# A 2048-token decoder trunk on one core: FFN input loaded eighth by eighth, weight sums moved ahead, and the loads of the down projection taken apart from their splits

## The chip, the cores and the metric

One NeuronCore of a Trainium2 chip. The metric is the time of one execution in microseconds of device time. The kernel before takes 2434.5 us, the median of three runs (2428.35, 2434.5 and 2436.43).

## The reference

One layer on a sequence of 2048 tokens, width 1024, in float32: an input projection that feeds two kinds of heads (gated mixing in chunks of 128 tokens, and a matrix memory carried from chunk to chunk), an output projection with a residual, a feed-forward block with a causal convolution of three taps behind its up projection, a gated input embedding, and a last norm. What the change touches is the feed-forward block:

```python
h = rms_norm(x, g_ffn[i])
up = causal_dwconv(h @ w_up[i], ffn_conv_w[i], ffn_conv_b[i])   # 1024 -> 5632
a, bv = jnp.split(up, 2, axis=-1)
x = x + (jax.nn.silu(a) * bv) @ w_down[i]                       # 2816 -> 1024
gate = jax.nn.sigmoid(rms_norm(x, g_ple[i]) @ w_ple_gate[i])
x = x + gate * (p[i] @ w_ple[i])
return rms_norm(x, g_final)
```

## The kernel before

Every float32 product is made of three TensorE (PE) products of a rounded high half and the rest: high x high, high x low, low x high. So each operand is first split: ACT copies the high half, DVE subtracts it from the whole. The functions `wsplit`, `halves` (L738) and `split` (L744) do that.

**Phase one** (up to L696) takes the tokens in four blocks of 512, one after the other, some 220 us each. A block runs four token groups (the value, gate and output-gate weights `w_v`), the query, key and gate tiles (`qk_tile`, `u_tile`), the heads, and the output projection. A `qk_tile` ends with a convolution on DVE (tile `cv`, L526), a SiLU on ACT (L528), and the head that follows begins with PE's products `pm` (L536). The block's sum with the residual goes to a buffer in HBM, `x1s[b]`. During block b, `make_h` of the block before brings that result back in four parts of 512 KB (tile `xs`, L694), multiplies it by the norm (L231), and stores the FFN input (`td`). The even blocks store two quarters a part; the odd ones also load the even block's (`hs`, L238) and store the sums and differences from which the feed-forward block makes its products: it multiplies 2x2 blocks of matrices with 7 block products in place of 8, in the order `ORDER = (1, 2, 6, 5, 7, 3, 4)`. The tiles `xs` come from a pool of two, which the streams of the block input `xT` use as well. The weights of the down projection need such sums too, 11 pairs of rows (`sums_load`, `sums_make`, L252 to L266: two loads of 512 KB into tiles `ds0` and `ds1`, four DVE operations, four stores to `sd`).

**Phase two** keeps its tiles in rings (`SLOTS`): 28 of kind "k" and 7 "r" of 4 KB a partition, 4 "f", 2 large "w", 8 small "m", 4 "x". A ring's next tile waits until the last use of the one that it replaces is over. It runs `up_half(0)`, `down_half(0)`, `up_half(1)`, `down_half(1)`, each for half the tokens, and then the embedding (`Ple`) for the four blocks. An up half has 22 columns j with 7 steps each, a down half 7 products with 11 steps each; a step is 12 PE products of 128x512. `Steps.run` calls functions a number of steps ahead of the step that uses them:

```python
early = [(4, lambda prod=prod, k=k: o.load(prod, k)), (2, lambda prod=prod, k=k: o.prep(prod, k))]
if k == NK - 1 and prod in (2, 7, 3, 4):
    early.append((2, lambda prod=prod: o.fetch(*{2: (0, 0), 7: (1, 1), 3: (0, 1), 4: (1, 0)}[prod])))
```

In a down half, `load` brings weights and activations into an "x" tile (`sx`, L915 and L916), `prep` splits them (`dw`, `dt`), `fetch` brings a residual quarter (`xr`, L924, 1 MB into a "w" tile). Down half 0 also makes the inputs of the second up half (`build_t`: `hx` loads of 512 KB into "x" tiles, split into `tt`); down half 1 does the same with the gate weights (`w_pg`, tile `wst`, L995) and the embedding's input (`xg`, L1007, into "f" tiles).

A tile scheduler works out the instruction streams: each engine runs its own in order, and where the code doesn't pin an instruction (`tc.keep_in_program_order`), the scheduler places it by its own estimate of when its inputs are there. Loads are issued on SP in order, most stores on POOL. A load that has to wait for its tile holds up every load behind it on SP.

## Time and profile before

| | |
|---|---|
| profiled execution | 2437.65 us, of which the span of the trace is 2435.9 |
| PE busy | 2352.9 us (97%) |
| DVE busy | 1813.4 us (74%) |
| ACT busy | 1101.5 us (45%) |
| DMA, mean of the span | 157 GB/s |
| phase one | 0 to 872 us, blocks end at about 220, 430 and 650 |
| up half 0, down half 0 | 872 to 1323, 1323 to 1544 us |
| up half 1, down half 1 | 1544 to 1967, 1967 to 2195 us |
| embedding and last norm | 2195 to 2436 us |

PE's busy time counts a product from its start to its modelled end, at whatever clock the chip granted. So what the kernel loses against an unbroken stream of products is its idle time plus the stretches at a lower clock. The granted clock is given for a stretch as its mean: 1.00 is the upper of two levels, 2.4 GHz, 0.50 the lower, 1.2 GHz.

### The profile page before, as it was taken

Reading aid. Unit: us, or ns where it says so; the run is one execution under the profiler, and the core shown is the slowest. Engines: PE = TensorE matmul, PEld = TensorE weight load, DVE = VectorE, ACT = ScalarE, POOL = GpSimd, SP = SyncE. Lnnn points to the kernel's source line nnn. Section 1 sums busy time; section 2 is a strip of 40 time slices with the busy share of each in tenths; the row PEclk is TensorE's granted clock in tenths of the full one; section 3 lists DMA queues with packets and bytes.
Section 4 is the critical chain, followed back from the end, with each engine's and each line's share of the span. In section 5 each row is a group of like instructions: output and inputs, shape, how many; then the busy total and the mean of one; then the engine's idle time right before and its main releaser. Section 6 shows DMA issues by size and latency. Waiting matters only on the chain.

```text
span 2435.9 us, 31412 instructions
## 1 busy us (share of the span) xinstructions
PE 2352.9 (97%) x11336; PEld 1990.2 (82%) x11336; DVE 1813.4 (74%) x3107; ACT 1101.5 (45%) x1848; POOL 206.3 (8%) x339
## 2 busy tenths in 40 slices
PE   8999999989999989999999999999999998999998
PEld 8888987988798868787788777788888877888887
DVE  7787767677766669898897657788888866575666
ACT  4453265246326554444444555444444444553323
POOL 1100100020010101011110000010100000000000
PEclk9999999999999999999999999999999999999999
DMA  7626533572543254355554777332332467671111
GB/s 252 228 94 198 159 98 119 163 238 78 165 136 98 87 208 149 120 183 197 179 189 159 252 251 261 140 108 100 122 124 101 134 223 245 206 258 53 70 70 70
DMA packets 145245, 382.72 MB, mean 157 GB/s; under 512 B 17344, under 2 KB 19520, under 8 KB 144064
## 3 DMA queue, kind: packets, MB, share of 16 engines
q1 hardware_dynamic: 118704, 291.16, 36.8%
q0 software_dynamic: 26240, 89.15, 9.4%
q8 instruction: 89, 1.46, 0.2%
q14 instruction: 68, 0.56, 0.1%
q10 hardware_dynamic: 144, 0.40, 0.1%
HBM read 283.12 MB, written 97.52 MB: 156 GB/s over the span
## 4 chain that ended last, share of the span: by engine, by line
PE 68%; DMA 11%; DVE 11%; issue 6%; ACT 2%; POOL 1%; SPq 1%; DVEq 0%; POOLq 0%; ACTq 0%
PE ub L827 4%; PE ub L828 4%; PE ub L829 4%; DMA hx<-td 4%; PE acc L125 4%; PE acc L124 4%; PE acc L127 4%; PE ua L827 3%; PE ua L828 3%; PE ua L829 3%; PE gt L124 3%; PE gt L125 3%; PE gt L127 3%; PE acc L371 3%; PE acc L373 3%
## 5 line engine op out<-in xcount | busy, mean ns | idle before, releaser
L827 PE MATMUL ub<-tt,sw 128*128 128x512 f32 x704 | 275.9, 392 | 9.7 <-ACT tt L740 5.6
L828 PE MATMUL ub<-tt,sw 128*128 128x512 f32 x704 | 275.7, 392 | 2.8 <-DVE tt L741 2.8
L829 PE MATMUL ub<-tt,sw 128*128 128x512 f32 x704 | 274.9, 391 | 0.0
L746 ACT ACTIVATE sw<-wr 128x1024 fp32r<-128x1024 f32 x132 | 140.0, 1061 | 286.0 <-PE ua L828 239.3
L827 PE MATMUL ua<-tt,sw 128*128 128x512 f32 x528 | 208.0, 394 | 9.7 <-DVE ua L857 9.0
L828 PE MATMUL ua<-tt,sw 128*128 128x512 f32 x528 | 207.2, 392 | 0.0
L829 PE MATMUL ua<-tt,sw 128*128 128x512 f32 x528 | 206.9, 392 | 0.0
L117 DVE TENSOR_TENSOR wlo<-wst,whi 128x1024 fp32r<-128x1024 f32 (+2 forms) x144 | 158.5, 1103 | 41.6 <-PE acc L127 22.9
L371 PE MATMUL acc<-whi,hh 128*128 128x384 f32 (+1 forms) x512 | 173.4, 339 | 9.1 <-ACT hh L217 6.7
L372 PE MATMUL acc<-wlo,hh 128*128 128x384 f32 (+1 forms) x512 | 172.7, 338 | 0.0
L747 DVE TENSOR_TENSOR sw<-wr,sw 128x1024 fp32r<-128x1024 f32 x132 | 161.0, 1220 | 15.1 <-ACT sw L746 12.3
L373 PE MATMUL acc<-whi,hl 128*128 128x384 f32 (+1 forms) x512 | 172.1, 337 | 0.2 <-DVE hl L218 0.2
L827 PEld LDWEIGHTS ub<-tt,sw 128*128 128x128 f32 x704 | 133.0, 189 | 41.1 <-ACT tt L740 6.5
L828 PEld LDWEIGHTS ub<-tt,sw 128*128 128x128 f32 x704 | 132.8, 189 | 31.1 <-DVE tt L741 4.0
L829 PEld LDWEIGHTS ub<-tt,sw 128*128 128x128 f32 x704 | 132.9, 189 | 27.7
L939 PE MATMUL da<-dt,dw 128*128 128x512 f32 x352 | 140.0, 398 | 9.0 <-DVE dt L741 9.0
L938 PE MATMUL da<-dt,dw 128*128 128x512 f32 x352 | 138.9, 396 | 4.2 <-ACT dt L740 4.2
L741 DVE TENSOR_TENSOR dt<-sx,dt 128x512 fp32r<-128x512 f32 x154 | 105.9, 688 | 47.9 <-ACT dt L740 47.6
L741 DVE TENSOR_TENSOR dw<-sx,dw 128x512 fp32r<-128x512 f32 x154 | 105.8, 687 | 46.2 <-ACT dw L740 45.9
L940 PE MATMUL da<-dt,dw 128*128 128x512 f32 x352 | 139.0, 395 | 0.0
L740 ACT ACTIVATE dw<-sx 128x512 fp32r<-128x512 f32 x154 | 95.9, 623 | 82.0 <-DMA sx<-w_down 27.6
L740 ACT ACTIVATE dt<-sx 128x512 fp32r<-128x512 f32 x154 | 96.1, 624 | 70.2 <-PE db L940 31.8
(339 smaller groups left out, 5737.5 us busy)
## 6 DMA issues: line engine op xcount, KB each, us to landing
wr<-w_up SPq DMA_DIRECT2D x44, 512.0 KB, 3.7
wr<-w_up SPq DMA_DIRECT2D x88, 256.0 KB, 4.9
act<-fc POOLq DMA_DIRECT2D x44, 512.0 KB, 5.7
ad<-two POOLq DMA_DIRECT2D x88, 256.0 KB, 4.9
sx<-sd SPq DMA_DIRECT2D x88, 256.0 KB, 4.1
sx<-ad SPq DMA_DIRECT2D x88, 256.0 KB, 4.3
wst<-w_v SPq DMA_DIRECT2D x48, 384.0 KB, 3.2
sx<-w_down SPq DMA_DIRECT2D x66, 256.0 KB, 4.4
```

The costliest lines, as they stand in the source:

```text
L124: PE.matmul(ps, wh, mh, start=(i == 0), stop=False)
L125: PE.matmul(ps, wh, ml, start=False, stop=False)
L127: PE.matmul(ps, wl, mh, start=False, stop=(i == n - 1))
L371: PE.matmul(ps[t][:, :n], a_h, rh, start=(k == 0), stop=False)
L372: PE.matmul(ps[t][:, :n], a_h, rl, start=False, stop=False)
L373: PE.matmul(ps[t][:, :n], a_l, rh, start=False, stop=(k == KD - 1))
L740: A.activation(t[:, :HALF], x, AF.Copy)
L741: V.tensor_tensor(t[:, HALF:], x, t[:, :HALF].bitcast(F32), ALU.subtract)
L747: V.tensor_tensor(lo, x, hi.bitcast(F32), ALU.subtract)
L827: PE.matmul(ps, hi[:, c], t[:, :HALF], start=first, stop=False, skip_group_check=on)
L828: PE.matmul(ps, hi[:, c], t[:, HALF:], start=False, stop=False, skip_group_check=on)
L829: PE.matmul(ps, lo[:, c], t[:, :HALF], start=False, stop=last, skip_group_check=on)
```

## The change

The FFN input of a block is now loaded and made in separate functions, each called for one of the four parts (`ffn_load`, `ffn_make`), spread by `ffn_at` over token group 2 and 3 and the tiles behind. It goes through the tiles `ds0` (the block's result) and, in odd blocks, `ds1` (the even block's quarters), of which there is one each and which the weight sums use as well. All 11 weight sums are made in phase one (`SUMS_T`, `turn`); the five in up half 0 are gone. In the down halves, the loads of `hx` go into "m" tiles, 256 KB each and 4 steps ahead, the residual into two "f" tiles, 4 steps ahead, the gate weights into "f" tiles, 5 steps ahead, and the embedding's input of even blocks into "w" tiles, 9 steps ahead; their splits are pinned at their step. The embedding's loads for the next block are called at tile 3, the splits at tile 6.

```diff
+SUMS_T = {1: 0, 2: 1, 3: 2, 0: 3}
...
             for i in range(2):
                 ST.dma_start(t[1 + i][:, kk, :], xs[:, i, :])
             return
-        hs = pair()
-        for i in range(2):
-            DMA.dma_start(hs[:, i, :], t[1 + i][:, kk, :])
         ST.dma_start(t[3][:, kk, :], xs[:, 1, :])
         t5, t7, t6, t4 = one(), one(), one(), one()
         V.tensor_tensor(t7, xs[:, 1, :], xs[:, 0, :], ALU.subtract)
...
             rB = nq.rB
+            if b == NB - 1:
+                sums_load(SUMS_T[0], ds_tile)
 
...
                 nx.st1()
 
+            if b == NB - 1:
+                sums_make(SUMS_T[0])
+            if b:
+                sums_load(SUMS_T[b], ds_tile)
             ps = tok_group(1, {0: [chain1], 1: [chain2], 2: [chain3]} | ({3: [pend[0].st2]} if b else {}))
...
+            if 0 < b:
+                sums_make(SUMS_T[b])
+            ffn_at0 = pend[1](0) if b else None
             ps = tok_group(2, ({2: [nx.st2]} if b + 1 < NB else {}) | ({1: [pend[0].st3]} if b else {}))
...
+            ffn = {}
+
+            def ffn_at(kk):
+
+                if b:
+                    if kk:
+                        pend[2](kk - 1, ffn[kk - 1])
+                    if kk < 4:
+                        ffn[kk] = pend[1](kk)
+
             if b:
-                pend[1]()
+                ffn[0] = ffn_at0
+            ffn_at(1)
...
             k1, o0 = qk_tile(5, lambda f: head_b(*a, f))
+            ffn_at(2)
...
             k2, o1 = qk_tile(6, lambda f: head_b(*a, f))
+            ffn_at(3)
...
             k3, o2 = qk_tile(7, lambda f: head_b(*a, f))
+            ffn_at(4)
...
             nf = SumSq(tp, "t", NT, V)
-            turn = {1: {3: 0}, 2: {3: 1}, 3: {1: 2, 3: 3, 5: 4, 7: 5}}.get(b, {})
+            turn = {0: {4: 4}, 1: {4: 5}, 2: {4: 6}, 3: {1: 7, 3: 8, 5: 9, 7: 10}}.get(b, {})
             for d in range(-2, KD):
...
                 nf.st1()
 
-            def make_h(b=b, nf=nf):
-                for kk in range(4):
-                    xs = xpool.tile([P, 2, TB], F32, tag="xs", name="xs")
-                    DMA.dma_start(xs, x1s[b][:, kk::4, :])
-                    ffn_in(b, kk, xs, nf.rB, lambda: xpool.tile([P, 2, TB], F32, tag="xs", name="hs"), lambda: tt("hx"))
-            pend = (nf, make_h)
+            def ffn_load(kk, b=b):
+                t = ds_tile(0), (ds_tile(1) if b % 2 else None)
+                DMA.dma_start(t[0], x1s[b][:, kk::4, :])
+                if b % 2:
+                    for i in range(2):
+                        DMA.dma_start(t[1][:, i, :], tds[b // 2][1 + i][:, kk, :])
+                return t
+
+            def ffn_make(kk, t, b=b, nf=nf):
+                ffn_in(b, kk, t[0], nf.rB, t[1], lambda: tt("hx"))
+            pend = (nf, ffn_load, ffn_make)
...
-        def halves(x, tag, nm):
+        def keep(ins, pin=True):
+            if pin:
+                tc.keep_in_program_order(ins)
...
             T[prod, kk] = halves(raw_t[prod][:, kk % 2, :], "k", "tt")
+
+        def load_t(s, prod, kk):
+            raw_t[prod, kk] = slot("m", "hx")
+            DMA.dma_start(raw_t[prod, kk], tds[s][prod][:, kk, :])
+
+        def make_t(prod, kk):
+            T[prod, kk] = halves(raw_t.pop((prod, kk)), "k", "tt", True)
 
 
         class Up:
...
 
             def fetch(self, fh, th):
-                self.x = [pairs(slot("w", "xr")[:, 0:2048])]
-                DMA.dma_start(self.x[0], x1s[2 * self.s + th][:, 4 * fh:4 * fh + 4, :])
+                self.x = [pairs(slot("f", "xr")) for _ in range(2)]
+                for q in range(2):
+                    DMA.dma_start(self.x[q], x1s[2 * self.s + th][:, 4 * fh + 2 * q:4 * fh + 2 * q + 2, :])
 
             def mm(self, prod, k):
                 if k == 0:
...
             def give(self, fh, th, bank, plus):
                 b = 2 * self.s + th
-                n, x = n3[b], self.x[0]
+                n = n3[b]
                 for q in range(2):
-                    xq = x[:, 2 * q:2 * q + 2, :]
+                    xq = self.x[q]
                     V.tensor_tensor(xq, xq, bank[q], ALU.add)
                     if plus is not None:
                         V.tensor_tensor(xq, xq, plus[q], ALU.add)
...
                     if k == NK - 1 and prod in (2, 7, 3, 4):
-                        early.append((2, lambda prod=prod: o.fetch(*{2: (0, 0), 7: (1, 1), 3: (0, 1), 4: (1, 0)}[prod])))
+                        early.append((4, lambda prod=prod: o.fetch(*{2: (0, 0), 7: (1, 1), 3: (0, 1), 4: (1, 0)}[prod])))
                     early.extend(extra.get(i * NK + k, ()))
                     steps.add(lambda prod=prod, k=k: o.mm(prod, k), (lambda prod=prod: o.post(prod)) if k == NK - 1 else None, early)
 
 
...
-            st = slot("r", "wst")
-            DMA.dma_start(st, src)
-            return split(st, tag, "wg")
+        raw_w = {}
+
+        def load4(key, src, tag="r"):
+            raw_w[key] = slot(tag, "wst")
+            DMA.dma_start(raw_w[key], src)
+
+        def split4(key, tag, pin=False):
+            return split(raw_w.pop(key), tag, "wg", pin)
 
         class Ple:
             def __init__(self, i):
                 self.i, self.x, self.xp, self.h = i, [], [], []
 
-            def start(self, ds=range(KD)):
+            def load(self, ds=range(KD)):
                 i = self.i
                 for d in ds:
...
-                        DMA.dma_start(self.xp[-1], x2s[i][:, d:d + 2, :])
-                    x = self.xp[-1][:, d % 2, :]
+                    if d % 2:
+                        continue
+                    if i % 2:
+                        t = slot("x", "xg")
+                    elif d in (0, 6):
+                        self.wt = slot("w", "xw")
+                        t = self.wt[:, 0:1024]
+                    else:
+                        t = self.wt[:, d * 512:d * 512 + 1024]
+                    self.xp.append(pairs(t))
+                    DMA.dma_start(self.xp[-1], x2s[i][:, d:d + 2, :])
+
+            def start(self, ds=range(KD), pin=False):
+                for d in ds:
+                    x = self.xp[d // 2][:, d % 2, :]
                     h = slot("k", "hg", F32R)
-                    A.activation(h[:, :TB], x, AF.Copy, scale=c1(C_GPLE + d))
-                    V.scalar_tensor_tensor(h[:, TB:], x, c1(C_GPLE + d), h[:, :TB].bitcast(F32), ALU.mult, ALU.subtract)
+                    keep(A.activation(h[:, :TB], x, AF.Copy, scale=c1(C_GPLE + d)), pin)
+                    keep(V.scalar_tensor_tensor(h[:, TB:], x, c1(C_GPLE + d), h[:, :TB].bitcast(F32), ALU.mult,
+                                                ALU.subtract), pin)
...
-                t = slot("w", "pp", F32R)
...
+                self.p = split(self.praw, "f", "pp", pin)
...
             at(8 + 2 * kk, 5, lambda kk=kk: last_in(kk))
-        for i, k in enumerate(range(6, NK)):
-            at(11 + 2 * i, 2, lambda k=k: sums_load(k, lambda i: pairs(slot("x", "ds"))))
-            at(11 + 2 * i, 3, lambda k=k: sums_make(k))
         up_half(0, ex)
 
         ex = {}
         for i, (prod, kk) in enumerate((p, k) for p in ORDER for k in range(4)):
-            ex.setdefault(8 + 2 * i if i < 24 else 44 + i, []).append((0, lambda prod=prod, kk=kk: build_t(1, prod, kk)))
+            ex.setdefault(8 + 2 * i if i < 24 else 44 + i, []).extend([
+                (4, lambda prod=prod, kk=kk: load_t(1, prod, kk)), (0, lambda prod=prod, kk=kk: make_t(prod, kk))])
         down_half(0, ex)
 
         ex = {}
...
         def pg(d):
-            wpg[d] = split4(w_pg[d], "k")
+            wpg[d] = split4(d, "k", True)
+
+        def step(i, *fns):
+            ex.setdefault(i, []).extend((0, f) for f in fns)
 
         for d in range(KD):
-            ex.setdefault(6 + 4 * d, []).append((0, lambda d=d: pg(d)))
-            ex.setdefault(40 + 3 * d, []).append((0, lambda d=d: ple[0].start((d,))))
-        ex.setdefault(70, []).append((0, ple[0].start_p))
+            step(4 + 4 * d, lambda d=d: load4(d, w_pg[d], "f"))
+            step(9 + 4 * d, lambda d=d: pg(d))
+            if d % 2 == 0:
+                step(33 + 3 * d, lambda d=d: ple[0].load((d,)))
+            step(42 + 3 * d, lambda d=d: ple[0].start((d,), True))
+        step(66, ple[0].load_p)
+        step(72, lambda: ple[0].start_p(True))
         down_half(1, ex)
         steps.run()
 
-        wpe.extend(split4(w_pe[k], "r") for k in range(2))
+        for k in range(2):
+            load4(("e", k), w_pe[k])
+        wpe.extend(split4(("e", k), "r") for k in range(2))
         fin = None
         for b in range(NB):
...
                 hooks[3] = [fin.st3, done]
             if b + 1 < NB:
+                o = ple[b + 1]
+                hooks.setdefault(3, []).extend([o.load_p, o.load])
                 hooks.setdefault(4, []).append(n3[b + 1].st2b)
-                hooks.setdefault(5, []).extend([n3[b + 1].st3, ple[b + 1].start_p, lambda b=b: ple[b + 1].start(range(4))])
+                hooks.setdefault(5, []).append(n3[b + 1].st3)
+                hooks.setdefault(6, []).extend([o.start_p, lambda o=o: o.start(range(4))])
                 fin, = ple[b].run(hooks)
                 ple[b + 1].start(range(4, KD))
                 continue
...
```

On DVE, in block 1, the part of the stream that scales the FFN input. Before (`xs` are the loaded parts, `lrs` and `gv` belong to a layer norm, `wlo` are low halves of weights, `cv` the convolution of a query or key tile):

```order
453 L231 SCALAR_TENSOR_TENSOR xs<-xs,col,rB 128x512
454 L478 BN_AGGR mu<-bnst 128x2
455 L477 BN_STATS bnst<-gv 128x6
456 L115 CAST whi<-wst 128x768
457 L478 BN_AGGR mu<-bnst 128x2
458 L231 SCALAR_TENSOR_TENSOR xs<-xs,col,rB 128x512
459 L480 TENSOR_SCALAR lrs<-mu 128x4
460 L117 TENSOR_TENSOR wlo<-wst,whi 128x768
461 L231 SCALAR_TENSOR_TENSOR xs<-xs,col,rB 128x512
462 L483 TENSOR_SCALAR gv<-gv,mu,lrs 128x512 x4
463 L231 SCALAR_TENSOR_TENSOR xs<-xs,col,rB 128x512
464 L117 TENSOR_TENSOR wlo<-wst,whi 128x1024 x2
```

and now (the numbered `ds` are successive contents of the two tiles; L261 begins a weight sum):

```order
443 L118 TENSOR_TENSOR wlo<-wst,whi 128x1024
444 L232 SCALAR_TENSOR_TENSOR ds_3352<-ds_3352,col,rB 128x512 x2
445 L118 TENSOR_TENSOR wlo<-wst,whi 128x1024
446 L378 TENSOR_SCALAR osig<-acc 128x384 x2
447 L232 SCALAR_TENSOR_TENSOR ds_3581<-ds_3581,col,rB 128x512
448 L118 TENSOR_TENSOR wlo<-wst,whi 128x1024
449 L232 SCALAR_TENSOR_TENSOR ds_3581<-ds_3581,col,rB 128x512
450 L118 TENSOR_TENSOR wlo<-wst,whi 128x1024
451 L544 SCALAR_TENSOR_TENSOR cv<-ub,col,cv 128x512 x3
452 L532 COPY ub<-qhalo 128x3
453 L118 TENSOR_TENSOR wlo<-wst,whi 128x1024
454 L261 TENSOR_TENSOR ds_4074<-ds_4073,ds_4074 128x512
```

Before, all eight multiplies stood ahead of the first tiles' weights (`wlo` of 1024 columns). Now the last two parts and a weight sum, which all pass through the one tile `ds0`, stand in this stretch, and the key tile's convolution follows behind the sum's first operations, in rows 456, 458 and 460. In the stream of loads on SP, each of the two parts and the sum's load stands ahead of weights of the query, key and gate tiles.

On SP, where the first down half begins. Before (`sx` with the input `act_8` is the activation load of step 4 of the half):

```order
257 L924 DMA xr<-x1s_81 128x2048
258 L915 DMA sx<-w_down 128x512
259 L916 DMA sx<-act_0_115 128x512
260 L915 DMA sx<-w_down 128x512
261 L916 DMA sx<-act_2_117 128x512
262 L915 DMA sx<-w_down 128x512
263 L916 DMA sx<-act_4_119 128x512
264 L915 DMA sx<-w_down 128x512
265 L916 DMA sx<-act_6_121 128x512
266 L924 DMA xr<-x1s_82 128x2048
267 L915 DMA sx<-w_down 128x512
268 L916 DMA sx<-act_8_123 128x512
```

and now:

```order
267 L952 DMA sx<-w_down 128x512
268 L953 DMA sx<-act_4_119 128x512
269 L952 DMA sx<-w_down 128x512
270 L953 DMA sx<-act_6_121 128x512
271 L829 DMA wr<-w_up 128x1024
272 L830 DMA wr<-w_up 128x512
273 L831 DMA wr<-w_up 128x512
274 L816 DMA hx<-td_1_96 128x512 x4
275 L816 DMA hx<-td_2_97 128x512 x4
276 L962 DMA xr<-x1s_81 128x1024 x2
277 L952 DMA sx<-w_down 128x512
278 L953 DMA sx<-act_8_123 128x512
```

Eight loads of `hx` and both halves of the residual now stand ahead of step 4's load. The second of the two goes into the "f" tile that the last column's multiply (L906, before L869) still reads.

## Rows read from the trace of the kernel before

**Rows 1.** Busy us by engine (with instruction counts), PEclk, DMA share, GB/s: two stretches.
```profile
220.00:430.00 210.00, 206.56 (x1129) 183.61 (x1128) 149.60 (x349) 99.35 (x205) 19.26 (x23) 1.00 0.44 141
1323.00:1544.00 221.00, 215.29 (x927) 173.81 (x926) 146.00 (x214) 118.10 (x201) 5.36 (x10) 0.99 0.72 242
```

**Rows 2.** The same table for five stretches with lost PE time.
```profile
1079.00:1200.00 121.00, 111.59 (x472) 90.37 (x471) 105.05 (x125) 49.46 (x69) 23.14 (x43) 0.96 0.58 205
100.00:130.00 30.00, 25.92 (x141) 21.06 (x140) 24.70 (x56) 12.57 (x28) 3.24 (x6) 1.00 0.58 205
525.00:550.00 25.00, 17.75 (x86) 14.78 (x86) 19.67 (x28) 12.49 (x20) 5.40 (x10) 0.83 0.87 306
1960.00:1985.00 25.00, 21.05 (x88) 17.03 (x87) 15.67 (x23) 8.36 (x13) 2.16 (x4) 0.94 0.47 159
1985.00:2060.00 75.00, 67.26 (x278) 53.54 (x278) 42.51 (x60) 36.76 (x61) 1.07 (x2) 0.95 0.75 263
```

**Rows 3.** PE's waits of the whole span: us in total, times, longest us.
```profile
PE pm L536 <- ACT qk L528: 10.6, 5, 7.2
PE da L939 <- DVE dt L741: 9.0, 5, 5.1
PE ua L827 <- DVE ua L857: 9.0, 3, 4.3
```

**Rows 4.** Timeline of DVE, block 2: start, us, instruction, idle before and its releaser.
```profile
526.22 1.42 DVE L231 SCALAR_TENSOR_TENSOR xs<-xs,col,rB 128x512 f32<-128x512 f32 x2 [6.72 <-DMA xs<-x1s]
535.96 1.41 DVE L231 SCALAR_TENSOR_TENSOR xs<-xs,col,rB 128x512 f32<-128x512 f32 x2 [3.52 <-DMA xs<-x1s]
```

**Rows 5.** Chain of waits in block 0, 80 to 130 us: start, us, what.
```profile
83.83 4.90 DMA sd<-ds
88.81 4.77 DMA ds<-w_down
...
113.94 5.35 DMA sd<-ds
119.34 3.92 DMA ds<-w_down
```

**Rows 6.** Chain of waits in up half 0, 1079 to 1200 us.
```profile
1097.07 4.89 DMA ds<-w_down
...
1179.93 7.29 DMA ds<-w_down
```

**Rows 7.** Timelines of POOL, DVE and PE in block 1.
```profile
295.24 0.54 POOL L234 DMA_DIRECT2D td<-xs  x1 [0.91 <-DVE lrs L480]
...
316.91 2.33 DVE L526 SCALAR_TENSOR_TENSOR cv<-ub,col,cv 128x512 f32<-128x512 f32 x3 [2.84 <-ACT cv L524]
...
326.75 0.39 PE L536 MATMUL pm<-qk 128*128 128x128 f32 x2
```

**Rows 8.** Timelines of SP, PE and DVE where the down halves begin.
```profile
1322.58 0.33 SPq L915 DMA_DIRECT2D sx<-w_down  x1
1323.17 0.39 PE L938 MATMUL da<-dt,dw 128*128 128x512 f32 x1
1328.81 1.22 DVE L869 TENSOR_TENSOR fc<-fc 128x1024 f32<-128x1024 f32 x1
...
1955.02 19.41 SPq L1007 DMA_DIRECT2D xg<-x2s  x2
...
1982.43 1.22 PE L938 MATMUL da<-dt,dw 128*128 128x512 f32 x2 [3.94 <-ACT dt L740]
```

**Rows 9.** DMA issues of the whole span: count, KB each, median us to landing.
```profile
wr<-w_up SPq DMA_DIRECT2D x44, 512.0 KB, 3.7
wr<-w_up SPq DMA_DIRECT2D x88, 256.0 KB, 4.9
...
sx<-act SPq DMA_DIRECT2D x66, 256.0 KB, 4.9
...
xs<-x1s SPq DMA_DIRECT2D x12, 512.0 KB, 5.9
```

More of the change, by code (lines that the diff above doesn't have):

```diff
@@ L225, in stream, with ffn_in @@
                 fn(k + i, xs[:, i, :])
-    def ffn_in(b, kk, xs, rB, pair, one):
+    def ffn_in(b, kk, xs, rB, hs, one):
         t = tds[b // 2]
@@ L736, in __call__, with halves, split @@
                 return self.t[:, (self.i - 1) % 2, :]
-        def halves(x, tag, nm):
+        def keep(ins, pin=True):
+            if pin:
+                tc.keep_in_program_order(ins)
+        def halves(x, tag, nm, pin=False):
             t = slot(tag, nm, F32R)
-            A.activation(t[:, :HALF], x, AF.Copy)
-            V.tensor_tensor(t[:, HALF:], x, t[:, :HALF].bitcast(F32), ALU.subtract)
+            keep(A.activation(t[:, :HALF], x, AF.Copy), pin)
+            keep(V.tensor_tensor(t[:, HALF:], x, t[:, :HALF].bitcast(F32), ALU.subtract), pin)
             return t
-        def split(x, tag, nm):
+        def split(x, tag, nm, pin=False):
             hi, lo = slot(tag, nm, F32R), slot(tag, nm, F32R)
-            A.activation(hi, x, AF.Copy)
-            V.tensor_tensor(lo, x, hi.bitcast(F32), ALU.subtract)
+            keep(A.activation(hi, x, AF.Copy), pin)
+            keep(V.tensor_tensor(lo, x, hi.bitcast(F32), ALU.subtract), pin)
             return hi, lo
@@ L991, in trunk_kernel @@
         wpg, wpe = {}, []
-        def split4(src, tag):
-            st = slot("r", "wst")
-            DMA.dma_start(st, src)
-            return split(st, tag, "wg")
+        raw_w = {}
[4 more added lines that the diff above has]
+            return split(raw_w.pop(key), tag, "wg", pin)
         class Ple:
@@ L1093, in last_in @@
             DMA.dma_start(xs, x1s[NB - 1][:, kk::4, :])
-            ffn_in(NB - 1, kk, xs, nl.rB, lambda: pairs(slot("f", "hl")), Twos())
+            hs = pairs(slot("f", "hl"))
+            for i in range(2):
+                DMA.dma_start(hs[:, i, :], tds[NH - 1][1 + i][:, kk, :])
+            ffn_in(NB - 1, kk, xs, nl.rB, hs, Twos())
         ex = {}
```

12 lines of the change are left out of this document (4 added, 8 removed).

## The prediction, written before the changed kernel ran

> **What bounds the kernel now.** PE does, and the views are read in the order of that question. The page's first table says that PE is busy 97% of the span, DVE 74%. So the change can't shorten PE's work, which stays the same; it can only take away or add moments in which PE waits, and the lower clock that follows a long wait. The list of PE's waits [rows 3] names whom it waits for: the SiLU of a key tile (10.6 us, one wait alone 7.2), the low half of an operand in the down halves (9.0 us in five), and an addition on DVE in an up half (9.0 us in three). The table by stretches says where these lie and at what clock [rows 1, 2]. It is to be read as length less PE's busy time; a mean clock of 0.83 means that PE had the lower of its two levels for 2 x 0.17 of the stretch. A quiet stretch shows what is reachable: block 1 is 210 us long and PE idle for 3.4 of them at clock 1.00 [rows 1]. Last, timelines and the chain of waits say who came last in each loss [rows 4 to 8].
>
> **The change part by part.** The sum starts at the profiled execution, 2437.65 us: its span of 2435.9 and 1.75 around it.
>
> *FFN input in block 2 (odd).* In 525 to 550 PE is busy 17.75 of 25 us at clock 0.83 [rows 2]. DVE stood for 6.72 and 3.52 us on loads of the block's result [rows 4], because all four parts were asked for at once through two tiles, and the key tile's convolution stood behind them. Now each part is asked for some 6 us of DVE work ahead of its use, and its four operations stand apart in the stream. The idle 7.25 us go, and of the 2 x 0.17 x 25 = 8.5 us at the lower level that part in which PE worked: between 0 and 4.2 us, I take 2.2. Gain 9.5, from 7 to 11.
>
> *FFN input in blocks 1 and 3 (even).* These blocks lose next to nothing now [rows 1]. The change puts their parts through one tile, `ds0`. The next load may start only when both stores of the part before have landed. The trace shows such a round trip in block 0, where weight sums go through `ds0` the same way: store 4.90 and load 4.77, or 5.35 and 3.92, so 9.3 to 9.7 us [rows 5]. For the parts themselves the median load is 5.9 us [rows 9]. I take 9.2 us. In block 1 the stores of the second part are issued at 295.24 [rows 7]. The third part lands at 304.4 and its two multiplies (0.71 each by [rows 4]) end at 305.9. The fourth lands at 315.6; with two multiplies and two weight halves between, DVE is at 318.5. The weight sum that is next in `ds0` lands at 327.7. The convolution of the key tile comes behind its first operations: two of the sum and three of the convolution, about 4.5 us with those between, end at 332.2. ACT and the first product of the head follow within 1 to 2 us: 333.7. In the trace of before that convolution began at 316.91 and the head at 326.75 without a wait [rows 7]. So PE is 7 us late. A wait of that length brings the lower clock, as at 525 to 550 [rows 2]; I add 1 us for it, as part of the wait may be taken earlier, on weights. Each microsecond in the round trip counts three times. At 8 us the loss is 3.4, at 10.5 us some 11 and 2 for the clock. Cost 8 a block, from 3 to 13, and block 3 has the same rows in the same order: 16 together.
>
> *Weight sums out of up half 0 and thinner in block 0.* In 1079 to 1200 PE loses 9.4 us at clock 0.96 [rows 2]. The wait is for an addition on DVE [rows 3], and DVE is late because a sum's operations stand ahead of it, on loads of 4.89 to 7.29 us that themselves wait for an "x" tile [rows 6]. With the sums these waits go. The FFN input of the last block stays in the same stretch and shares tiles with the stores of the activation sums, so I leave 1 us. For the clock (2 x 0.04 x 121 = 9.7 us at the lower level) up to 4.8 come on top, I take 2.6. Gain 11, from 8 to 13. In block 0 two sums remain of six; the round trips there [rows 5] are what PE's 4.1 idle us in 100 to 130 [rows 2] go back to. Gain 3.5, from 2 to 4. The moved sums' four DVE operations each (0.7 us) fall into blocks with DVE busy 71% [rows 1]; beyond the round trips counted above I charge 1 us, from 0 to 6, since two more of the sums in block 1 and four in block 3 pass through the same tiles.
>
> *Loads ahead in down half 0.* Now an `hx` load is called at the step that splits it, and its wait holds DVE and through it PE. The half loses 221 - 215.3 = 5.7 us at clock 0.99, so up to 2.2 more [rows 1]. Some 0.9 us of it is the start. With the load four steps (11 us) ahead, twice a landing of about 5 us [rows 9], the rest goes: gain 7, from 3 to 8.
>
> *A wait at its start.* The second load of the residual needs the "f" tile that the last multiply of the up half reads, and stands ahead of step 4's loads on SP. That multiply ended at 1328.81 + 1.22 = 1330.0; step 4's loads were issued at 1322.58 [rows 8]. Step 4 is due at 1323.17 + 4 x 12 products of 0.232 us (215.29 us for 927 [rows 1]) = 1334.3. Issued at 1330.4, the second load at 1330.8, landing 4.9 later [rows 9], at 1335.7, then two copies on ACT and two subtractions, about 2 us: 1337.7. PE waits 3.4 us, and 1 for the clock. Cost 4.5, from 0 (if the loads land in 2 us less and the splits overlap) to 6. That such a wait does this is in the trace: where down half 1 begins, SP stood for two loads of 19.41 us in all on the same kind of tile, and PE waited 3.94 us [rows 8].
>
> *Down half 1.* There the order of the loads changes but the wait doesn't: now the second gate-weight load needs the last multiply's tile. So the 3.95 idle us of 1960 to 1985 [rows 2] stay. What goes is the in-line loads of gate weights and of the embedding's input in 1985 to 2060: 7.74 us idle at clock 0.95 [rows 2]. Gain 6.5, from 3 to 9.
>
> *The embedding.* Loads at tile 3 and splits at tile 6 in place of both at 5: nothing, plus or minus 1; PE waits there on the norm's row sums, which are not moved.
>
> Gains 9.5 + 11 + 3.5 + 7 + 6.5 = 37.5, costs 16 + 1 + 4.5 = 21.5, net 16. 2437.65 - 16 = 2421.65 for a profiled execution. This profile lies 3.15 us above the median of the runs shown, so I forecast 2418.5 us.
>
> **A rule that speaks against the change.** One tile, filled and emptied in turn, is what blocks 1 and 3 pay for, by the 9.3 to 9.7 us of [rows 5]. The Trainium skill, "Trainium Kernel Development and Optimization", section Best Practices, asks for double buffers so that loads run beside the work; the change goes from two tiles to one there, and the trace of before agrees with the rule by those rows. Without the single tile the sum would be 16 us lower, which is the first rival.
>
> **The rivals.**
> *No new waits in phase one: 2402.5.* If DVE runs late there anyhow, or the three weight buffers and the idle time of DVE before the head absorb three round trips, the 16 us go. For it: before, the key tile's convolution was done at 319.24, 7.5 us ahead of the head [rows 7]. Against it: my propagation has used that slack already.
> *The down halves are held by the DMA engines: 2432.* Down half 0 moves 242 GB/s with the engines busy 0.72 of the time [rows 1], and 1985 to 2060 has 0.75 [rows 2]. If loads called earlier only queue longer, the 13.5 us of both halves don't come: 2418.5 + 13.5. Against it: in 525 to 550 the engines reached 0.87 and 306 GB/s [rows 2], so there is room. The Trainium skill, "SBUF — State Buffer", section on the DMA setup-cost knee, gives each transfer a fixed cost of about 2 us and asks for large ones; the change cuts the `hx` and residual loads in half. The trace doesn't show smaller loads to be cheaper: 256 KB landed in 4.9 us where 512 KB took 3.7 [rows 9].
> *Slower: the round trips of `ds0` empty the weight buffers: 2446.* Place: blocks 1 and 3, on SP, where loads of weights stand behind each load into `ds0`. A load took 7.29 us [rows 6] and a store 5.35 [rows 5]; with 12.6 us a round trip, three of them are 10 us later than at 9.2, 18 a block, and the sums that follow in the same tile, two more in block 1 and three in block 3, add another round trip's excess of 3 to 6 us each block. That is 2 x 22 + 4.5 + 1 of costs against 37.5 of gains, 12 worse than none, or 2446. It decides from about 11.5 us a round trip, where the costs reach the gains.
>
> **How the numbers follow.** Forecast as worked out, 2418.5 with its own range of 2408 to 2429: 0.50. No new waits: 0.17. Down halves bound by DMA: 0.13. Slower: 0.12. The rest, 0.08, lies between these on either side. The range takes the costs at their lower ends (6 + 0 + 0) with the gains as they are for the low side, 2437.65 - 31.5 - 3.15 = 2403, less 2 for the clock: 2401; on the high side it holds the DMA case with the costs of blocks 1 and 3 some 5 above mine: 2437. What a measurement can tell from no change is about 0.3%, 7.3 us: faster means below 2427.2. The forecast gives 0.46 of its 0.50, no new waits all, DMA-bound 0.03, the rest 0.05: faster 0.71. Within: 0.04 + 0.09 + 0.01 + 0.02 = 0.16. Slower 0.13.
>
> **What would show it.** Right: no wait of DVE above 2 us on loads of the FFN input in block 2, and PE's 7.25 us gone; in blocks 1 and 3 three waits of DVE of 4 to 8 us each, for loads into `ds0`, and a wait of PE at L536's counterpart of 5 to 10 us; up half 0 at most 3 us idle behind its first 20 us; down half 0 with a wait of 3 to 4 us at its fifth step and nothing above 1 us behind. Wrong: blocks 1 and 3 as long as before (first rival); down halves that lose as much, with landings of `hx` and `sx` above 7 us (second); blocks 1 and 3 longer by 15 us and more, with PE's waits on weights (third).

## The result, and the profile after

The changed kernel takes 2414.02 us, the median of four runs (2413.3 to 2414.91), against 2434.7 of the kernel before on the same chip: a ratio of 0.9923, 95% interval 0.9911 to 0.9935. Forecast were 2418.5. The profiled execution takes 2413.49 us with a span of 2411.8, 24.1 us less than that of before (which lay 3 us above its median, this one 0.5 below).

PE runs the same 11336 products in both kernels, stage by stage. So the start of the n-th product in one trace less its start in the other tells how far ahead a kernel is there, and the difference between two marks is what a stage gained. This is the forecast of each stage beside that, from the two profiled executions:

| stage | forecast | measured |
|---|---|---|
| block 0 | -3.5 | -0.9 |
| block 1 | +8 | +8.1 |
| block 2 | -9.5 | -6.9 (-9.6 in 525 to 550) |
| block 3 | +8 | +11.5 |
| up half 0 | -11 | -16.2 (-14.0 in 1079 to 1200) |
| down half 0 | +4.5 and -7 | +4.9 and -10.5 |
| up half 1 | 0 | -1.4 |
| down half 1 | -6.5 | -13.2 (-11.8 in 1985 to 2060) |
| embedding | 0 | +0.4 |
| all, with the 1 us charged for the moved sums | -16 | -24.2 |

One profile gives a single stage to some 2 us either way. The changed kernel and seven of the variants below have the same instruction streams up to 1300 us; over these eight profiles block 0 reads -0.8 to -3.1 (median -1.7), block 1 +6.5 to +10.2 (+7.4), block 2 -5.3 to -7.1 (-6.8), block 3 +7.9 to +11.5 (+9.9) and up half 0 -13.0 to -16.2 (-14.0).

The stretches that answer to [rows 1, 2] (the same table of busy time, with shifted bounds where the work has moved):

```profile
220.00:430.00 210.00, 201.98 (x1093) 179.30 (x1092) 150.81 (x351) 96.84 (x202) 21.54 (x29) 0.98 0.46 151
515.00:540.00 25.00, 25.00 (x123) 22.11 (x123) 15.82 (x23) 16.36 (x24) 2.85 (x4) 1.00 0.58 189
650.00:870.00 220.00, 212.06 (x1138) 188.12 (x1137) 146.95 (x331) 88.29 (x184) 30.91 (x47) 0.98 0.51 172
1085.00:1200.00 115.00, 114.78 (x506) 94.56 (x505) 105.52 (x122) 53.18 (x72) 17.75 (x33) 1.00 0.48 168
1318.00:1345.00 27.00, 23.36 (x96) 18.55 (x95) 17.00 (x22) 11.36 (x20) 2.15 (x4) 0.94 0.76 246
1984.00:2060.00 76.00, 76.00 (x337) 62.94 (x336) 50.49 (x71) 45.23 (x72) 1.07 (x2) 1.00 0.83 287
```

Three of the bad stretches of before have become full ones: PE 25 of 25, 114.78 of 115 and 76 of 76 us, at clock 1.00. Two quiet ones have become worse: block 1 idles 8.0 us now at 0.98, and the beginning of down half 0 3.6 us. The list of PE's waits shows the exchange against [rows 3]:

```profile
PE acc L598 <- DVE hc L591: 10.7, 5, 2.8
PE pm L554 <- ACT qk L546: 10.4, 5, 3.9
PE da L976 <- ACT dt L770: 7.1, 2, 3.6
```

The head's wait for a key tile (now L554) sums to 10.4 us, hardly less than the 10.6 of before, but it is no longer one of 7.2 in block 2; the two longest are in blocks 1 and 3. The addition in up half 0 is not among the waits any more. This is DVE in block 1 (timeline: start, us, instruction, idle before and its releaser), as the prediction had propagated it from [rows 5, 7]:

```profile
302.43 1.42 DVE L232 SCALAR_TENSOR_TENSOR ds<-ds,col,rB 128x512 f32<-128x512 f32 x2 [3.44 <-DMA ds<-x1s]
313.14 0.75 DVE L232 SCALAR_TENSOR_TENSOR ds<-ds,col,rB 128x512 f32<-128x512 f32 x1 [7.23 <-DMA ds<-x1s]
...
324.57 0.69 DVE L261 TENSOR_TENSOR ds<-ds,ds 128x512 f32<-128x512 f32 x1 [4.04 <-DMA ds<-w_down]
...
328.44 0.75 DVE L544 SCALAR_TENSOR_TENSOR cv<-ub,col,cv 128x512 f32<-128x512 f32 x1
```

The loads came at 302.4, 313.1 and 324.6 (forecast 304.4, 315.6 and 327.7; the block began 0.9 us earlier), and the convolution ended at 329.2 (forecast 332.2). PE then waits for the head, here and at the same place in block 3, where a weight sum at the block's beginning has cost some more before:

```profile
329.90 0.49 PE L554 MATMUL pm<-qk 128*128 128x128 f32 x2 [3.91 <-ACT qk L546]
...
675.17 0.54 PE L370 MATMUL acc<-wlo,hh 128*128 128x392 f32 x1 [2.58 <-DVE wlo L118]
...
767.68 0.80 PE L554 MATMUL pm<-qk 128*128 128x128 f32 x2 [3.84 <-ACT qk L546]
```

Behind the wait of 3.91 the granted clock falls, and it falls once more at the end of the block, where PE waits 2.8 us for `hc`, a head's output behind its norm. The kernel before waits there too, 2.63 us, and keeps its clock. These are two stretches of the changed kernel and, last, the one of the kernel before:

```profile
330.00:335.00 5.00, 4.80 (x31) 3.75 (x31) 2.91 (x4) 4.97 (x10) 0.00 (x0) 0.66 0.88 304
410.00:415.00 5.00, 2.46 (x8) 2.08 (x9) 3.60 (x10) 1.57 (x4) 1.38 (x1) 0.76 0.35 105
...
405.00:410.00 5.00, 3.24 (x16) 2.50 (x17) 4.10 (x10) 1.95 (x3) 1.37 (x1) 1.00 0.36 99
```

The wait of 2.58 is of the kind that the forecast had only charged 1 us for: DVE stood 7.70 us on a sum's load, with a block's first weights behind it.

```profile
672.95 0.69 DVE L261 TENSOR_TENSOR ds<-ds,ds 128x512 f32<-128x512 f32 x1 [7.70 <-DMA ds<-w_down]
```

And these are SP and PE where the two down halves begin, against [rows 8]:

```profile
1317.38 8.67 SPq L962 DMA_DIRECT2D xr<-x1s  x2
1326.10 0.42 SPq L952 DMA_DIRECT2D sx<-w_down  x1
...
1333.48 0.73 PE L976 MATMUL da<-dt,dw 128*128 128x512 f32 x2 [3.64 <-ACT dt L770]
...
1943.64 19.43 SPq L1035 DMA_DIRECT2D wst<-w_pg  x2
...
1970.55 0.73 PE L976 MATMUL da<-dt,dw 128*128 128x512 f32 x2 [3.44 <-ACT dt L770]
```

The residual's second load holds SP until the last multiply is over; step 4's loads follow at 1326.10, and PE waits 3.64 us where 3.4 were forecast. In down half 1 the gate weights wait 19.43 us as the embedding's input did before.

### The profile page after: what moved, and what is told of

It is laid out like the page before. It is cut to its first block, busy times and chain, and to the rows that moved or that the text cites. A ratio compares the mean times of both kernels' runs of the same rounds, so it can differ in the third digit from the quotient of the medians.

```text
span 2411.8 us, 31443 instructions
## 1 busy us (share of the span) xinstructions
PE 2347.6 (97%) x11336; PEld 1992.5 (83%) x11336; DVE 1814.7 (75%) x3107; ACT 1106.5 (46%) x1850; POOL 206.3 (9%) x339
## 4 chain that ended last, share of the span: by engine, by line
PE 81%; DVE 7%; DMA 6%; issue 3%; ACT 1%; POOL 1%; SPq 0%; DVEq 0%; POOLq 0%; ACTq 0%
PE ub L864 6%; PE ub L865 6%; PE ub L866 6%; PE ua L864 4%; PE ua L865 4%; PE ua L866 4%; PE acc L125 3%; PE acc L126 3%; PE gt L125 3%; PE gt L126 3%; PE gt L128 3%; PE da L977 3%; PE acc L128 3%; PE da L978 3%; PE da L976 3%; PE acc L369 3%
## 5 line engine op out<-in xcount | busy, mean ns | idle before, releaser
L118 DVE TENSOR_TENSOR wlo<-wst,whi 128x1024 fp32r<-128x1024 f32 (+2 forms) x144 | 158.4, 1103 | 24.9 <-ACT whi L114 15.9
L777 DVE TENSOR_TENSOR sw<-wr,sw 128x1024 fp32r<-128x1024 f32 x132 | 161.2, 1221 | 15.1 <-ACT sw L776 12.3
L976 PE MATMUL da<-dt,dw 128*128 128x512 f32 x352 | 137.0, 391 | 7.1 <-ACT dt L770 7.1
L977 PE MATMUL da<-dt,dw 128*128 128x512 f32 x352 | 138.1, 392 | 0.3 <-DVE dt L771 0.2
L978 PE MATMUL da<-dt,dw 128*128 128x512 f32 x352 | 137.7, 391 | 0.0
L114 ACT ACTIVATE whi<-wst 128x1024 fp32r<-128x1024 f32 x80 | 84.2, 1058 | 93.0 <-PE acc L371 35.2
L771 DVE TENSOR_TENSOR dw<-sx,dw 128x512 fp32r<-128x512 f32 x154 | 105.7, 686 | 24.2 <-ACT dw L770 24.2
```

Source lines behind the costliest of these rows:

```text
L118: (leng or V).tensor_tensor(lo[:, :n], st[:, :n], hi[:, :n].bitcast(F32), ALU.subtract)
L771: keep(V.tensor_tensor(t[:, HALF:], x, t[:, :HALF].bitcast(F32), ALU.subtract), pin)
L777: keep(V.tensor_tensor(lo, x, hi.bitcast(F32), ALU.subtract), pin)
L976: PE.matmul(ps, w[:, c], t[:, :HALF], start=first, stop=False, skip_group_check=on)
L977: PE.matmul(ps, w[:, c], t[:, HALF:], start=False, stop=False, skip_group_check=on)
L978: PE.matmul(ps, w[:, HALF + d * 128:HALF + (d + 1) * 128], t[:, :HALF], start=False, stop=last, skip_group_check=on)
```

## The experiments

Each is one edit of the changed kernel (2414.02 us). What a stage gains or loses is read as above, from one profiled execution each.

**One: the multiplies of even blocks pinned.**

```diff
+            if b % 2 == 0:
+                tc.keep_in_program_order(ins)      # ins: the multiply of ffn_in
```

> The changed kernel, with the two multiplies of each part of the FFN input in the even blocks pinned behind what the code emits before them on DVE, so that the four parts stand one to each query or key tile and not in a row; loads, tiles and sums as in the change. Theory of the prediction (three round trips of ds0 in a row hold DVE ahead of the key tile's convolution): block 1 and block 3 each lose their wait of 3.9 us at the head and the lower clock behind it, some 5 us a block; ratio to the kernel before about 0.988, that is 2404 us, from 2400 to 2407. Rival (the blocks are longer because DVE and the DMA engines have more to do in them, wherever it stands): the waits move to a later tile and the time stays at 2414 within 3 us.

2420.16 us (2416.72 to 2423.01), ratio 0.9938 (0.9918 to 0.9957). Both theories missed the time, the first was right on the place: block 1 is as long as before the change (+0.1 in place of +8.1), and the head's wait in block 3 is gone (0 in place of 5.6 and 1.4). But the sums, which are not pinned, now stand elsewhere: 15.0 us are lost at the beginning of block 2, 7.2 at that of up half 0. Timeline of PE:

```profile
462.00 0.69 PE L371 MATMUL acc<-whi,hh 128*128 128x384 f32 x1 [6.72 <-DVE whi L116]
...
890.45 0.80 PE L866 MATMUL ub<-tt,sw 128*128 128x512 f32 x1 [7.82 <-ACT tt L772]
```

and of DVE ahead of the second, two sums in a row that wait for a round trip each:

```profile
869.81 0.69 DVE L263 TENSOR_TENSOR ds<-ds,ds 128x512 f32<-128x512 f32 x1 [6.72 <-DMA ds<-w_down]
882.26 0.69 DVE L263 TENSOR_TENSOR ds<-ds,ds 128x512 f32<-128x512 f32 x1 [7.25 <-DMA ds<-w_down]
```

**Two: the loads into "f" tiles pinned on SP.**

```diff
-                    DMA.dma_start(self.x[q], x1s[...])
+                    keep(DMA.dma_start(self.x[q], x1s[...]))
-            DMA.dma_start(raw_w[key], src)
+            keep(DMA.dma_start(raw_w[key], src), tag == "f")
```

> The changed kernel, with the loads of the residual and of the gate weights into the f tiles pinned on SP behind the loads emitted before them. Theory (these loads wait for the up half's last multiply and hold up step 4's loads behind them): the waits of PE of 3.64 us at 1333 and 3.44 us at 1970 go, with the lower clock behind each; 4 to 5 us each, so 9 us less than the change, 2405, ratio 0.988. Rival (step 4's loads wait for their own x tiles, which come free no earlier): at most 3 us less, 2411 to 2414.

2407.21 us (2404.29 to 2411.35), ratio 0.989 (0.9871 to 0.9909): 6.8 us less than the change by medians, between the theory (9) and the rival (at most 3), and nearer to the theory. Step 4's load of down half 0 is issued at 1319.23 and that of down half 1 at 1955.93, not held up any more; PE's wait in down half 1 shrinks from 3.44 to 0.68 us, and 1967 to 1985 gains 5.5 us where the change gained 1.4. In down half 0 this execution doesn't show it: PE's wait comes later, 2.60 us, and the first 37 us lose 4.0 in place of 4.8. In the kernels of four, eleven and twelve, with the same pins, these 37 us lose nothing. Timeline of PE:

```profile
1338.91 0.49 PE L976 MATMUL da<-dt,dw 128*128 128x512 f32 x1 [2.60 <-ACT dt L770]
...
1973.69 0.50 PE L976 MATMUL da<-dt,dw 128*128 128x512 f32 x1 [0.68 <-ACT dt L770]
```

**Three: five sums back in up half 0, the other six called where they were.**

```diff
-            turn = {0: {4: 4}, 1: {4: 5}, 2: {4: 6}, 3: {1: 7, 3: 8, 5: 9, 7: 10}}.get(b, {})
+            turn = {1: {3: 0}, 2: {3: 1}, 3: {1: 2, 3: 3, 5: 4, 7: 5}}.get(b, {})
...
+        for i, k in enumerate(range(6, NK)):       # in up half 0, as before
+            at(11 + 2 * i, 2, lambda k=k: sums_load(k, lambda i: pairs(slot("x", "ds"))))
+            at(11 + 2 * i, 3, lambda k=k: sums_make(k))
```

> The changed kernel, with the weight sums where they were before: six in phase one, five in up half 0 in x tiles; all else as in the change. Theory (up half 0 gained 16 us because its five sums left): up half 0 is 14 to 17 us longer than in the change, block 3 loses the wait of 4.4 us at its beginning (a sum's operation stands ahead of weights there), block 0 has the sums' waits back; in all 2420 to 2428. Rival (up half 0 gained because the embedding and down halves left x tiles to it, or by a better schedule): up half 0 within 5 us of the change.

2425.85 us (2422.99 to 2426.87), ratio 0.9962 (0.9949 to 0.9975). As the theory had it for up half 0 and block 3: between the 5388th and the 5858th product (1079 to 1200 us in the kernel before) this kernel is as slow as before (0.0, the change gained 14.0), the beginning of block 3 loses nothing (the change 4.4), and PE waits for the addition in up half 0 again:

```profile
PE ua L856 <- DVE ua L886: 9.7, 3, 3.8
```

Block 0, which the theory had slower again, is not: the scheduler puts the other six sums into blocks 1 to 3 (322 to 793 us), where in the kernel before all six were begun in block 0, ahead of 124 us.

**Four: all pins of one and two, and the sums' first operation pinned as well.**

```diff
-        V.tensor_tensor(q[:, 1, :], p[:, 1, :], q[:, 1, :], ALU.add)
+        tc.keep_in_program_order(V.tensor_tensor(q[:, 1, :], p[:, 1, :], q[:, 1, :], ALU.add))
```

> The changed kernel, with the multiplies of the FFN input in even blocks and the first operation of each weight sum pinned on DVE where the code emits them, and the loads of residual and gate weights into f tiles pinned on SP. Theory (an operation pulled ahead on DVE by the scheduler's estimate holds everything behind it until its real load lands, and pinning puts it where the load has landed): blocks 1 and 3 lose the 8.1 and 11.3 us that they gained over the kernel before, the down halves some 7 us together; 2414 - 19 - 7 = 2388, from 2382 to 2396, ratio 0.981. Rival (pinned sums push their stalls elsewhere, as the pinned multiplies did to the sums at the ends of blocks 1 and 3): no better than the kernel with pinned loads, 2404 to 2414.

2411.78 us (2410.45 to 2413.05), ratio 0.9903 (0.9888 to 0.9918). The time is the rival's. The beginning of block 3, its FFN parts and the starts of the down halves are as the theory had them, and block 1 costs 2.8 in place of 8.1; but the four sums that the code emits at the end of block 3 stand there in a row, and PE waits 14.25 us for the first operands of up half 0 (12.5 us lost); another 11.8 are lost in block 2, ahead of 525 us.

```profile
887.76 0.80 PE L866 MATMUL ub<-tt,sw 128*128 128x512 f32 x1 [14.25 <-ACT tt L772]
```

**Five to ten: which part of the edit won the down halves.** Six kernels, each with one part of it undone.

*Five.* Down half 0's input as before.

```diff
-                (4, lambda ...: load_t(1, prod, kk)), (0, lambda ...: make_t(prod, kk))])
+                (0, lambda ...: build_t(1, prod, kk))
```

> The changed kernel, with the second half's up input in down half 0 loaded as before: 512 KB into x tiles, at the step of the split, splits not pinned; all else as in the change. Theory (10.5 us behind the first steps of down half 0 are won by the loads ahead of pinned splits): down half 0 is 8 to 12 us longer, 2422 to 2426 in all. Rival (they were won because the residual left the w tiles and came earlier): within 3 us of the change.

2421.44 us (2419.05 to 2426.23), ratio 0.9951 (0.9936 to 0.9967). The half loses all of it: -0.4 behind its first steps where the change has -10.5. ACT's waits in 1320 to 1540 name it, in the kernel before (in 1323 to 1544), in this kernel and in the changed one:

```profile
ACT tt L740 <- DMA hx<-td: 40.5, 14, 5.0
...
ACT tt L770 <- DMA hx<-td: 38.7, 14, 4.5
...
ACT tt L770 <- DMA hx<-td: 2.6, 2, 1.4
```

On SP the products' own loads wait for a tile that an `hx` load still holds, first in this kernel, then in the changed one:

```profile
SPq L952 <- DMA hx<-td: 20.1, 8, 4.2
...
SPq L952 <- DMA hx<-td: 1.4, 3, 0.7
```

*Six.* Its splits unpinned.

```diff
-            T[prod, kk] = halves(raw_t.pop((prod, kk)), "k", "tt", True)
+            T[prod, kk] = halves(raw_t.pop((prod, kk)), "k", "tt")
```

> The changed kernel, with the splits of the second half's up input in down half 0 not pinned; loads into m tiles, four steps ahead, as in the change. If the 10.5 us behind the first steps of down half 0 come from the pins: 6 to 10 us longer, 2420 to 2424. If from the loads into m tiles ahead of their step: within 3 us of the change.

2413.92 us (2412.57 to 2420.56), ratio 0.9917 (0.9898 to 0.9936): -9.7. The pins do nothing here.

*Seven.* Its loads called at the step of their split.

```diff
-                (4, lambda prod=prod, kk=kk: load_t(1, prod, kk)),
+                (0, lambda prod=prod, kk=kk: load_t(1, prod, kk)),
```

> The changed kernel, with the loads of the up input in down half 0 called at the step of their split and not four steps ahead; m tiles and pinned splits as in the change. If the four steps are what wins the 10.5 us: 8 to 12 us longer, 2422 to 2426. If the m tiles are (they are free early, so that the scheduler issues the loads ahead anyway, and no x tile of the products' own loads is taken): within 3 us of the change, 2411 to 2417.

2412.09 us (2407.2 to 2415.78), ratio 0.9899 (0.9878 to 0.992): -9.4. The number of steps does nothing to the time either. SP issues the first seven loads from 1303.18 on, ahead of the half (eight from 1305.04 on in the change), as their "m" tiles come free. ACT still waits 15.5 us for `hx` later in the half, in six waits, with hardly a loss to PE. So the other tile is left as the cause: as an "x" tile, the load shares the four that the products' own loads go through, and each waits for the other. With the tile goes the size of a load, 512 KB or 256 KB, and which of the two it is was not separated (a wider ring of "x" tiles was not tried).

*Eight.* The splits of gate weights and embedding input unpinned.

```diff
-            wpg[d] = split4(d, "k", True)
+            wpg[d] = split4(d, "k")
-            step(42 + 3 * d, lambda d=d: ple[0].start((d,), True))
+            step(42 + 3 * d, lambda d=d: ple[0].start((d,)))
```

> The changed kernel, with the splits of the gate weights and of the embedding's first input in down half 1 not pinned; loads, tiles and steps as in the change. If the 11.8 us that the change won at 1985 to 2060 come from the pinned splits: down half 1 is 6 to 12 us longer, 2420 to 2426. If they come from the tiles (loads into f and w tiles that come free early, where before they took r tiles that products still read): within 3 us of the change, 2411 to 2417.

2412.38 us (2406.09 to 2417.21), ratio 0.9908 (0.9881 to 0.9935): -11.5 in 1985 to 2060, as the change: the pins do nothing here either.

*Nine.* The gate weights in "r" tiles, called five steps ahead.

```diff
-            step(4 + 4 * d, lambda d=d: load4(d, w_pg[d], "f"))
+            step(4 + 4 * d, lambda d=d: load4(d, w_pg[d]))
```

> The changed kernel, with the gate weights loaded into r tiles as before, at the steps of the change and with pinned splits. If the tiles are what won the 11.8 us of down half 1: 6 to 12 us longer, 2420 to 2426, less some 4 us at its start, since the load no longer waits for the last multiply's f tile. If the pins are: 2409 to 2414.

2419.5 us (2417.44 to 2421.06), ratio 0.9934 (0.9919 to 0.9949). By its time alone this would be the tile's doing (6 to 12 us, less 4), but it is not lost there: still -10.1 in 1985 to 2060. Of the 7.4 us between the two profiles 3.5 lie ahead of 1300 us, where the streams are the same. The start did not get its 4 us back (+0.9 in 1967 to 1985, the change -1.4), since now the next load for an "f" tile is in front and waits the same time:

```profile
1947.76 19.42 SPq L962 DMA_DIRECT2D xr<-x1s  x2
```

*Ten.* The gate weights wholly as before: "r" tiles, called at the step of the split, unpinned.

```diff
-            step(4 + 4 * d, lambda d=d: load4(d, w_pg[d], "f"))
-            step(9 + 4 * d, lambda d=d: pg(d))
+            step(6 + 4 * d, lambda d=d: pg(d))      # pg: load4(d, w_pg[d]), then split4
```

> The changed kernel, with the gate weights in down half 1 wholly as before: loaded into r tiles at the step of their split, not pinned; the embedding's input as in the change. If the 11.8 us at 1985 to 2060 come from loading the gate weights steps ahead: ACT waits 4 to 5 us on each again, 8 to 12 us longer than the change, 2422 to 2426. If from the embedding's input in w tiles, or from the residual in f tiles: within 3 us of the change.

2424.5 us (2421.75 to 2428.88), ratio 0.9961 (0.9943 to 0.998): -3.3 in place of -11.8, as the first theory had it. ACT's waits in 1970 to 2060 have the gate weights' loads at their head, as in the kernel before (18.6 us in five there); the change has none of them:

```profile
ACT wg L776 <- DMA wst<-w_pg: 16.4, 6, 4.8
```

So in down half 1 8.5 of the 11.8 us come from calling the gate weights' loads ahead, in "r" or in "f" tiles; with the "f" tiles the pins are not needed, and with the "r" tiles that was not tried. What the other 3.3 come from was not separated.

**Eleven and twelve: a kernel without the new waits.** Pins as in four (in eleven on all parts), and sums moved to block 0, which makes no FFN input.

```diff
+                else:                                # in ffn_at, block 0
+                    sums_make((7, 8, 9, 5)[kk - 1])
+                    sums_load((8, 9, 5, 6)[kk - 1], ds_tile)
-            turn = {0: {4: 4}, 1: {4: 5}, 2: {4: 6}, 3: {1: 7, 3: 8, 5: 9, 7: 10}}.get(b, {})
+            turn = {0: {4: 4}, 3: {1: 10}}.get(b, {})
```

> The changed kernel with pinned loads into f tiles, and with the multiplies of the FFN input (all blocks) and each weight sum's first operation pinned on DVE; six of the eleven sums are moved to block 0, where no FFN input is made, one to each tile, so that none is left at the end of blocks 1 and 2 and one in block 3. Theory (what the change loses in phase one is only operations that stand on DVE ahead of a load not yet landed, and sums bunched at the end of blocks): blocks 1 and 3 as before the change (8 and 11 us less than the change), block 0 within 3 us, nothing new at the borders of blocks, the down halves 6 us less: 2414 - 19 - 6 = 2389, from 2383 to 2397. Rival (round trips of ds0 and ds1 cost their time wherever they stand): 2403 or more.

2403.77 us (2401.81 to 2406.77), ratio 0.987 (0.9851 to 0.989). By the time the rival (2403 or more) has it, by the place neither: block 3 and the down halves are as the theory had them, but block 1 began with 8.7 us lost, and block 2 lost 7.8 behind the place where the change wins. At the end of block 0 the residual's loads come late, with the loads of two sums among them on SP. Twelve takes those sums away and pins, of the odd block's parts, only the first:

```diff
-            turn = {0: {4: 4}, 3: {1: 10}}.get(b, {})
+            turn = {2: {4: 4}, 3: {1: 10, 5: 6}}.get(b, {})
```

> As the kernel with all pins and sums moved to block 0, but with no sum at the end of blocks 0 and 1, where a sum's loads on SP stood ahead of the residual's loads (sum 4 at the end of block 2, sums 10 and 6 at that of block 3), and of the odd block's parts only the first pinned. Theory (what that kernel lost at the beginning of block 1, 8.7 us, and in block 2, 7.8, are loads of sums ahead of other loads on SP, and pinned parts that put four operations in one place): block 1 within 3 us of the kernel before, block 2 some 5 us less; 2404 - 11 = 2393, from 2386 to 2399. Rival (the sums cost about the same wherever they stand in phase one): 2400 to 2407.

2394.02 us (2391.18 to 2396.62), ratio 0.9833 (0.9818 to 0.9848): 20 us below the change, and the fastest of all. The time is the theory's (2393). Block 1 loses 0.1, block 2 wins 7.0 again, block 3 loses 5.7 (all at its end, where two sums are left), the down halves win 10.3 and 16.1.

## Why the prediction was right

The direction and most of the mechanisms came as forecast, seven of the nine stages within 3.5 us, and the time lies 4.5 us from it. The two sides erred together, and that is luck: by the table the gains are 49.1 us in place of 37.5, the costs 24.9 in place of 21.5. Between the two profiled executions the gain is 24.1 us in place of 16; by the medians it is 20.7, since the profile of before lies 3 us above its median and this one 0.5 below.

- *Even blocks.* The mechanism came, and experiment one shows the cause in it: with the multiplies elsewhere, the 8 us are gone. That block 1 agrees to 0.1 us is luck. The forecast was 7 us of a late head and 1 of the clock. The head is 4.2 us late by the count of products (PE's wait is 3.91, under the 5 to 10 named as a sign, and the first of DVE's three waits is 3.44, under 4), 2.4 are lost behind it at clock 0.66, and 1.6 come at the block's end, at a wait that the kernel before has too, at clock 0.76. For the clock the prediction had 1 us, for the block's end nothing. In the sum, 305.9 and 9.2 make 315.1, not 315.6. In block 3 the FFN parts cost 7.0 (forecast 8); the other 4.4 us are a sum at its beginning, which experiment three takes away (1.8 to 4.5 in the eight profiles). The step that was mis-sized is the 1 us charged for the moved sums.
- *Block 2.* The cluster gave 9.6, forecast 9.5. Behind it the block lost 2.7 us that no step had: the odd block's operations and stores lie beside the heads there, but that they cause it is not shown. *Block 0.* 5.2 us were won up to 125 us, and 4.3 lost behind, where PE's waits for `hc` have grown (4.4 us in the block, before 2.3) and the clock is 0.83 in 170 to 180 and in 190 to 200 (before 1.00). Sums don't cause it: experiment three has none in block 0 and loses 3.9 there. The cause stays open.
- *Up half 0.* 14.0 in 1079 to 1200, forecast 11 (-13.0 to -16.2 for the stage in the eight profiles), and by experiment three all of it is the sums'. The 1 us left for the last block's input was not there, and I had taken 2.6 of up to 4.8 for the clock.
- *Down halves.* The start of half 0 came as forecast (+4.9); experiment two moves it by the order on SP alone, and in four, eleven and twelve, with the same order, it is 0.0. The rests were mis-sized: 10.5 against 7, and 11.8 against 6.5. For half 1 the prediction took 6.5 of 7.74 idle us and nothing for the clock of 0.95, without a reason; 11.8 came, 8.5 of it by the gate weights (experiment ten). For half 0 the measure itself was too small. Idle time plus the lower clock gave 7.9 us [rows 1]. But a product's modelled end is later than the moment when the next could start (it takes 0.39 us [rows 8], where in an unbroken stretch one starts every 0.2255), so a short wait leaves part of itself in the busy time. Counting products is better: the unbroken stretch 1984 to 2060 after the change has 337 in 76 us, 0.2255 each; the 927 of [rows 1] would take 209.0, so 12.0 us of the 221 were lost. For 1079 to 1200 and 1985 to 2060 [rows 2] the same count gives 14.6 and 12.3, and 14.0 and 11.8 came.
- *The reason given for the gain in half 0*, loads four steps ahead of pinned splits, was half wrong: the loads do come ahead, but neither the steps nor the pins do it (six, seven); the other tile does, with the smaller load in it. And it is ACT, not DVE, that waits for them.
- *The rivals.* No new waits in phase one: refuted by the rows above and by experiment one. Down halves held by the DMA engines: refuted, they ran 1984 to 2060 at 0.83 busy and 287 GB/s without a wait of PE. The slower rival: in block 1 the loads came 10.7 and 11.4 us apart with 1.5 us of multiplies between, so the round trips took 9.2 to 9.9 us, less than the 11.5 from which it decides.

## What to carry to other kernels

Where a scheduler fills an in-order queue by its own estimate of a load's landing, ask of each moved operation what stands behind it if the load comes later; one tile that is stored, loaded and computed in turn makes every further use late by a whole round trip. A cure that pins one of the operations moves the wait to the next that isn't pinned, and it took pins and another place for the sums to be rid of it. Size a loss by counting what the stretch should have issued at the pace of an unbroken one, and let the whole of it go when its cause goes.

## What was not expected of the hardware

More traffic in less time did not make the loads later. In 1984 to 2060 the DMA engines are busy 0.83 and move 287 GB/s, against 0.75 and 263 in the like stretch of before [rows 2]; yet in that stretch the products' weights land sooner at the median. First two rows of before (1985 to 2060), then two of the changed kernel:

```profile
sx<-w_down SPq DMA_DIRECT2D x15, 256.0 KB, 5.2
sx<-sd SPq DMA_DIRECT2D x11, 256.0 KB, 5.7
...
sx<-sd SPq DMA_DIRECT2D x20, 256.0 KB, 4.5
sx<-w_down SPq DMA_DIRECT2D x8, 256.0 KB, 5.0
```
